# A two-layer diffusion block on one core: score matmuls in another order, FFN weights tied behind the attention's steps, down factors inside the up product, modulation and squares swapped

## The chip, the cores and the metric

The kernel runs on 1 core of a Trainium2 chip. The metric is the device time of one execution in microseconds (us). Before the change the median of 3 runs is 2509.74 us (2507.56 to 2510.74).

## What is computed

Two layers over 1024 latent tokens and 256 context tokens of width 1024. Each layer: RMS norm and modulation, one input projection, then windowed attention (8 query heads on 2 key heads, keys of the own block of 128 and its two neighbours, all 256 context keys and one sink per head) next to a Fourier mixing of 512 channels, an output projection, norm and gated residual; then norm and modulation again, a SwiGLU FFN of width 2816, norm and gated residual. Layer 1 updates the latent tokens alone. Cut to what matters here:

```python
mod_lat = silu(c) @ w_ada[i] + b_ada[i]                  # shifts, scales, gates, for latent
mod_ctx = silu(c_ctx) @ w_ada[i] + b_ada[i]              # and for context tokens
h = modulate(rmsnorm(x, norm_pre_mix[i]), sh1, sc1)
p = h @ w_in[i]                                          # q, k, v, u; q and k rotated
logits = concat([q @ k_window * scale + mask, q @ k_ctx * scale, sink])
attn = softmax(logits)[..., :-1] @ concat([v_window, v_ctx])
four = real(fft2(u)) @ w_four
x_mid = x + g1 * rmsnorm(concat([attn, four]) @ w_out[i])
hf = modulate(rmsnorm(x_mid, norm_pre_ffn[i]), sh2, sc2)
x = x_mid + g2 * rmsnorm((silu(hf @ w_gate[i]) * (hf @ w_up[i])) @ w_down[i])
```

## The kernel before

Activations lie transposed in the chip's memory (channels on the 128 partitions, tokens along the row), in two token blocks, A and B (640 tokens each in layer 0, 512 in layer 1). Every product is made of two-part numbers, three matmuls for one: in the projections and the attention in a 32-bit format, in the FFN in float16. The FFN's up product is done as seven half-size products for eight (a Strassen-Winograd form), so that each of the 22 weight matrices of 128 hidden columns (11 of gate, 11 of up) is first turned into sums of its quarters.

**Who sets the order.** The program is written as Python generators which yield after each piece of work; `mix` takes a next piece from the generator whose share done, relative to the number given beside it, is lowest. A larger number thus spreads a generator's steps more tightly. The order so written is a priority only: a scheduler with a model of time reorders each engine's instructions and hands out the buffers of the pools. On the chip each engine then executes its own queue in order. `high_priority(offset=AHEAD_OF)` lets maximum, exponential and casts of the attention go ahead of work that is written earlier.

**Attention.** `attn` steps through pairs of heads. `score` (L191) writes the logits of one head into a two-bank tile (pool `sc`, two such tiles): the sink's column, the window in high and low part with two triangular masks of 128x128, the context in two parts. VectorE takes the maximum (`ng`, L215), ScalarE the exponential with its sum (`A`, `su`, L216). `turn` transposes the result on TensorE (`tp`, L226), and ScalarE (L230) and VectorE (L231) split it; `value` (L234) takes the reciprocal of the sums (L238, 128x128 after a broadcast) and multiplies with V (`pv`, L244). Beside it run `fill` (remaining projections, Fourier, first half of the output projection), in layer 0 also `work` (modulation by matmuls, L568) and `early`: `norms` (squares of 8 weight matrices, L448) and `ahead`, which makes the float16 parts of these 8 matrices and stores them in memory (`wc`). `sums` (L456) does that: high part on ScalarE (`wa` or `ww`, L464), low part on VectorE (L465), sums of quarters on VectorE (`raw`, L476 to L479).

**FFN.** 44 matrices' products (`matrix`, L1084) in three parts of `mix`. First beside residual, norms and operands of block B (`side`), then beside `down_norms` (24 loads of the down weights and their squares, L1158 and L1159), then beside the modulation of the next layer for the first and second third (`mod(0, 1)`, products with reduction on VectorE, L645, loads `wm` on SyncE's queue) and the squares of its first weights. From the fifth matrix pair on, weights are fresh: loaded into the pool `raw` (four tiles), squared, made by `sums`, used for both blocks. L1088 to L1115 evacuate a matrix's banks; L1120 to L1132 scale and split the hidden values. Behind the up product `down_scale(0)` (L1164) makes the factors `dn` of the down weights for block A: VectorE (L1169 to L1173), TensorE and VectorE in `highest` (L602, L603, L605), VectorE (L409 to L411, L1175). The down product (L1215) needs its weights `wd` from ScalarE (L1207) and VectorE (L1208) with that factor. Layer 1's first projection runs beside norm statistics (`nps` L667, `nr` L679, `rps` L689) and scaling of block B.

## Time and profile before

| | us |
|---|---|
| median of 3 runs | 2509.74 |
| the profiled execution | 2504.05 |
| its span, first to last instruction | 2502.2 |
| TensorE busy in it | 2352.4 |
| VectorE busy | 1787.2 |
| ScalarE busy | 1344.7 |

The stages in the span: layer 0's attention about 130 to 535 us, its FFN 576 to 1113, its down product to 1422; layer 1's projection and attention 1422 to 1780, its FFN 1827 to 2244, its down product to the end. TensorE's busy time counts each matmul with its run through the array, modelled, and matmuls overlap; so the distance from start to start is the better measure of one. The granted clock is TensorE's, as a share of full speed. A row of a wait names who waits, on whom, us in total, how many times, and the longest.

### The profile page before, as it was taken

What the parts mean: (1) busy time and instruction counts of PE and PEld (TensorE: products, weight loads), DVE (VectorE), ACT (ScalarE), POOL (GpSimd) and SP (SyncE); (2) the same over time, 40 slices, a digit from 0 to 9 for tenths busy, and PEclk for the clock granted to TensorE, in tenths of its full rate; (3) what the DMA queues carried; (4) which work ended last, traced back from release to release, by engine and by line L of the source; (5) the groups of instructions that cost most, each with busy time, mean ns of one, the idle gap of its engine ahead of it and who ended that gap; (6) DMA issues with size and microseconds to landing.
All of it is one profiled execution on the core that took longest, in us unless ns stands there. A gap on an engine that the chain in (4) does not pass through costs nothing. (4 is left out here: it accounts for less than half of the span.)

```text
span 2502.2 us, 44066 instructions
## 1 busy us (share of the span) xinstructions
PE 2352.4 (94%) x17224; PEld 1900.2 (76%) x17224; DVE 1787.2 (71%) x3462; ACT 1344.7 (54%) x2587; POOL 196.6 (8%) x204
## 2 busy tenths in 40 slices
...
GB/s 309 206 102 167 160 98 107 184 236 284 203 185 148 108 129 165 156 192 373 269 246 129 91 123 47 35 18 51 186 338 222 161 72 69 77 142 208 132 254 125
DMA packets 157377, 406.83 MB, mean 163 GB/s; under 512 B 17488, under 2 KB 34288, under 8 KB 157168
## 3 DMA queue, kind: packets, MB, share of 16 engines
...
## 5 line engine op out<-in xcount | busy, mean ns | idle before, releaser
L1084 PE MATMUL p<-ffn,ww 128*128 128x320 f16 (+1 forms) x7392 | 921.9, 287 | 25.5 <-ACT ww L464 5.5
L1084 PEld LDWEIGHTS <-ww 128*128 128x128 f16 x7392 | 722.7, 98 | 220.8 <-issue 23.5
L1215 PEld LDWEIGHTS <-wd 128*128 128x128 f16 x3696 | 363.6, 99 | 164.0 <-ACT wd L1207 5.8
L1215 PE MATMUL acc<-hid,wd 128*128 128x320 f16 (+2 forms) x2544 | 335.4, 294 | 3.5 <-ACT wd L1207 3.2
L1208 DVE SCALAR_TENSOR_TENSOR wd<-raw,dn,wd 128x256 f16<-128x256 f32 x440 | 186.4, 480 | 132.6 <-ACT wd L1207 132.0
L1207 ACT ACTIVATE wd<-raw,dn 128x256 f16<-128x256 f32 x440 | 187.2, 496 | 146.0 <-PE acc L1215 87.2
L518 PE MATMUL accn<-arena,hi 128*128 128x320 f32 (+1 forms) x992 | 252.2, 327 | 5.6 <-DVE X L259 2.0
L518 PE MATMUL acc<-arena,hi 128*128 128x320 f32 (+2 forms) x928 | 209.0, 330 | 5.6 <-ACT X L1038 3.8
L1215 PE MATMUL acc<-X,wd 128*128 128x320 f16 (+1 forms) x1152 | 195.0, 331 | 0.9 <-ACT wd L1207 0.9
L518 PEld LDWEIGHTS accn<-arena,hi 128*128 128x128 f32 x992 | 173.2, 190 | 16.3 <-DVE arena L231 2.7
L518 PEld LDWEIGHTS acc<-arena,hi 128*128 128x128 f32 x928 | 154.8, 190 | 23.4 <-ACT X L1038 5.3
L518 PE MATMUL accn<-arena,lo 128*128 128x320 f32 (+1 forms) x496 | 159.8, 325 | 1.7 <-DVE lo L400 1.7
L674 POOL TENSOR_TENSOR nr<-nm,mhalf 128x5 f32<-128x5 f32 (+2 forms) x17 | 18.2, 1069 | 1708.0 <-DVE nm L673 1708.0
L465 DVE SCALAR_TENSOR_TENSOR ww<-raw,sp,ww 128x1024 f16<-128x1024 f32 x112 | 125.4, 1147 | 27.3 <-ACT ww L464 27.1
L464 ACT ACTIVATE ww<-raw,sp 128x1024 f16<-128x1024 f32 x112 | 109.9, 1033 | 59.4 <-DVE raw L479 51.0
L400 DVE TENSOR_TENSOR lo<-raw,hi 128x1024 fp32r<-128x1024 f32 x77 | 101.6, 1320 | 55.0 <-ACT hi L399 39.9
L230 ACT CAST arena<-tp 128x512 fp32r<-128x512 f32 (+1 forms) x184 | 96.6, 528 | 76.6 <-PE tp L226 74.2
L216 ACT ACTIVATE A<-score,ng 128x641 f32<-128x641 f32 (+2 forms) x144 | 106.6, 741 | 46.9 <-PE tp L226 30.1
L215 DVE TENSOR_REDUCE ng<-score 128x1 f32<-128x641 f32 (+2 forms) x144 | 106.3, 740 | 28.6 <-PE score L208 27.3
L518 PE MATMUL acc<-arena,lo 128*128 128x320 f32 (+2 forms) x464 | 125.0, 327 | 0.1
L399 ACT CAST hi<-raw 128x1024 fp32r<-128x1024 f32 x77 | 80.6, 1047 | 75.1 <-PE acc L518 28.7
L448 ACT ACTIVATE junk<-raw 128x1024 bf16<-128x1024 f32 x88 | 92.3, 1051 | 42.1 <-DMA raw<-in_wup 19.2
(231 smaller groups left out, 3724.4 us busy)
## 6 DMA issues: line engine op xcount, KB each, us to landing
...
```

Of the source, the lines that this page charges most:

```text
L215: nc.vector.tensor_reduce(self.ng[:, hs], sv, axis=AX.X, op=ALU.max, negate=True)
L216: nc.scalar.activation(p, sv, AF.Exp, bias=self.ng[:, hs], accum_out=self.su[:, hs])
L230: nc.scalar.copy(ph, tp[:, 0:256 * n])
L400: nc.vector.tensor_tensor(lo[:, 0:w], raw[:, 0:w], hi[:, 0:w].bitcast(F32), op=ALU.subtract)
L448: self.nc.scalar.activation(junk[:], raw[j][:], AF.Square, accum_out=self.ss[:, j, i:i + 1])
L464: nc.scalar.activation(hi, src, AF.Copy, scale=s)
L465: nc.vector.scalar_tensor_tensor(lo, src, s, hi, op0=ALU.mult, op1=ALU.subtract)
L518: self.nc.tensor.matmul(ps, wt[:, ks], xt[:, a:b], start=(k == 0 and i == 0), stop=(k == n - 1 and i == 2))
L1084: nc.tensor.matmul(ps, w[:, at:at + P], G[:, k, x, c, 0:h], start=(start and k + t == 0), stop=(k == KD // 2 - 1 and t == 2), skip_group_c ...
L1207: nc.scalar.activation(wt[:, 0, c], raw[:, c], AF.Copy, scale=r)
L1208: nc.vector.scalar_tensor_tensor(wt[:, 1, c], raw[:, c], r, wt[:, 0, c], op0=ALU.mult, op1=ALU.subtract)
L1215: nc.tensor.matmul(out, wt[:, e, k], xs[x][:, s, u:v], start=(f + s + i == 0), stop=(f == NP - 1 and s == 1 and i == 2))
```

## The change

Seven things, in one diff. In `score` the long products come first, then the context's, then the masks, then the sink. The reciprocal is taken of the 128x2 sums, and a copy broadcasts it. Each score notes its maximum and its exponential (`urgent`), and with `issue_after` the squares, the high parts with their store, the low parts and the quarter sums of FFN weights that are written beside the attention are put behind them in ScalarE's and VectorE's order; `sums` now yields between its parts, with a further step between load and first use. `down_scale(0)` is called inside the up product, ahead of the last matrix's third product, so that its squares must be complete by then. `mod(0)` stands in the FFN's second part where `down_norms` stood; `down_norms` stands in the third with `mod(1)`. In layer 1's first projection the statistics of block B get the weight 9 for 14. The pace of the early weights follows the new number of steps (12 for 8 beside the attention, 28 of 40 steps for 16 of 24 beside down).

```diff
@@ score
-        nc.tensor.matmul(s[:, 511 - w:512 - w], net.bf1[:], net.sink[:, self.l, hd:hd + 1], start=True, stop=True)
         if w:
             loc = s[:, 512 - w:512]
             ls = slice(C + P * self.k0, C + P * self.k1)
             nc.tensor.matmul(loc, q, net.KHI[g][:, ls], start=True, stop=False)
-            if n > 0:
-                nc.tensor.matmul(loc[:, 0:P], net.bf[:, 0:P], net.bf[:, P:2 * P], start=False, stop=False)
-            if n < NB - 1:
-                nc.tensor.matmul(loc[:, w - P:w], net.bf[:, 0:P], net.bf[:, 2 * P:3 * P], start=False, stop=False)
-            nc.tensor.matmul(loc, q, net.KLO[g][:, ls], start=False, stop=True)
+            nc.tensor.matmul(loc, q, net.KLO[g][:, ls], start=False, stop=False)
         nc.tensor.matmul(s[:, 512:512 + C], q, net.KHI[g][:, 0:C], start=True, stop=False)
         nc.tensor.matmul(s[:, 512:512 + C], q, net.KLO[g][:, 0:C], start=False, stop=True)
+        if w:
+            if n > 0:
+                nc.tensor.matmul(loc[:, 0:P], net.bf[:, 0:P], net.bf[:, P:2 * P], start=False, stop=(n == NB - 1))
+            if n < NB - 1:
+                nc.tensor.matmul(loc[:, w - P:w], net.bf[:, 0:P], net.bf[:, 2 * P:3 * P], start=False, stop=True)
+        nc.tensor.matmul(s[:, 511 - w:512 - w], net.bf1[:], net.sink[:, self.l, hd:hd + 1], start=True, stop=True)
...
         with net.tc.high_priority(offset=AHEAD_OF):
-            nc.vector.tensor_reduce(self.ng[:, hs], sv, axis=AX.X, op=ALU.max, negate=True)
-            nc.scalar.activation(p, sv, AF.Exp, bias=self.ng[:, hs], accum_out=self.su[:, hs])
+            top = nc.vector.tensor_reduce(self.ng[:, hs], sv, axis=AX.X, op=ALU.max, negate=True)
+            exp = nc.scalar.activation(p, sv, AF.Exp, bias=self.ng[:, hs], accum_out=self.su[:, hs])
+        net.urgent = top.ins, exp.ins
@@ value
-            nc.vector.reciprocal(self.out[:, 0].rearrange("p (h d) -> p h d", h=2), self.su[:].unsqueeze(2).broadcast_to([P, 2, HD]))
+            nc.vector.reciprocal(self.su[:], self.su[:])
+            nc.vector.tensor_copy(self.out[:, 0].rearrange("p (h d) -> p h d", h=2), self.su[:].unsqueeze(2).broadcast_to([P, 2, HD]))
@@ norms
-            self.start(l, i)
+            raw = self.load(l, i)
             yield
+            self.squares(l, i, raw)
@@ squares, behind
+            with self.behind(1):
+                self.nc.scalar.activation(junk[:], raw[j][:], AF.Square, accum_out=self.ss[:, j, i:i + 1])
...
+    def behind(self, e):
+        return self.tc.issue_after(self.urgent[e]) if self.urgent else nullcontext()
@@ sums
-        parts(0, raw[0][:])
-        parts(1, a22)
+        one = high(0, raw[0][:]), high(1, a22)
         yield
-        nc.vector.tensor_tensor(a22, a21, a22, op=ALU.add)
...
-        parts(2, raw[0][:])
+        for e in one:
+            low(*e)
+        with self.behind(0):
+            nc.vector.tensor_tensor(a22, a21, a22, op=ALU.add)
...
         yield
-        parts(3, raw[1][:])
+        two = high(2, raw[0][:]), high(3, raw[1][:])
+        yield
+        for e in two:
+            low(*e)
         yield
@@ ffn_up
+                if n == 2 and m == (1, NP - 1, 1):
+                    self.down_scale(0)
@@ program
-                mix((self.inproj(l, 0, (1, 0, 2, 3, 4, 5)), cost(6, KD, BW - C)), (side, 14))
+                mix((self.inproj(l, 0, (1, 0, 2, 3, 4, 5)), cost(6, KD, BW - C)), (side, 9))
...
-            mix((fill, FILL[l]), (self.attn(l, queries), ATT[l]), (work, 17), (early, 8 * AHEAD))
+            mix((fill, FILL[l]), (self.attn(l, queries), ATT[l]), (work, 17), (early, 12 * AHEAD))
+            self.urgent = None
...
-            mix((part(up, 14 * AHEAD - 7), 2 * AHEAD * one), (self.down_norms(l), 24))
-            mix((up, one * (44 - 4 * AHEAD)), (mod(0, 1), 64), (iter(()) if last else self.norms(l + 1), 2 * AHEAD))
-            self.down_scale(0)
+            mix((part(up, 14 * AHEAD - 7), 2 * AHEAD * one), (mod(0), 32))
+            mix((up, one * (44 - 4 * AHEAD)), (self.down_norms(l), 30), (mod(1), 32),
+                (iter(()) if last else self.norms(l + 1), 2 * AHEAD))
...
-                mix(down(0, 0, w, first), (part(pre, 4 * AHEAD), 4 * AHEAD), (side, 32))
+                mix(down(0, 0, w, first), (part(pre, 7 * AHEAD), 7 * AHEAD), (side, 32))
```

How this moves the instructions shows at three places; the lines are those of each kernel's own file.

ScalarE in layer 0's attention, before: a weight's high part (`wa`) stands between two exponentials (`A,su<-score`) of a pair, and elsewhere ahead of a cast (`arena_391<-tp`).

```order
L867 CAST qs<-X 64x2x128 x2
L216 ACTIVATE A,su<-score,ng 128x641
L230 CAST arena_391<-tp 128x256
L464 ACTIVATE wa<-raw,sp_111 128x512
L216 ACTIVATE A,su<-score,ng 128x641
L469 DMA wc<-wa 128x512
L399 CAST hi<-raw 128x1024
L838 COPY X<-accn 128x320
L230 CAST arena_391<-tp 128x512
L257 COPY pvl<-pv 64x128 x2
L464 ACTIVATE wa<-raw,sp_111 128x1024
L230 CAST arena_391<-tp 128x512
```

The same engine and stage in the changed kernel (L218 is the exponential, L233 the cast, L479 the high part):

```order
L218 ACTIVATE A,su<-score,ng 128x641
L233 CAST arena_391<-tp 128x256
L218 ACTIVATE A,su<-score,ng 128x641
L479 ACTIVATE wa<-raw,sp_111 128x1024 x2
L404 CAST hi<-raw 128x1024
L482 DMA wc<-wa 128x1024 x2
L233 CAST arena_391<-tp 128x512
```

The high parts now come two at a time, directly behind the second exponential of a pair.

VectorE at the end of layer 0's up product, before: the reduction `hx` for block A's factors stands behind the last matrix's evacuations and maximum (`hm`), and the factors `dn_118` behind those of block B.

```order
L1115 SCALAR_TENSOR_TENSOR A<-p_11396,inv_122,A 128x320
L1103 TENSOR_TENSOR A<-A,p_11397 128x320
L1107 SCALAR_TENSOR_TENSOR A<-A,inv_122 128x960
L1120 TENSOR_REDUCE hm<-A 128x1
L603 TENSOR_REDUCE hx<-fps 1x1
L1121 TENSOR_SCALAR hm<-hm 128x1
L1122 TENSOR_SCALAR he<-hm 128x1
L1123 TENSOR_SCALAR hp<-he 128x1
L1169 TENSOR_SCALAR dn_119<-he 128x11
L409 TENSOR_SCALAR pe<-fps 128x1
```

The same in the changed kernel (L628 is `hx`, L1202 the factors, L1116 the evacuation of the last matrix's second product, L1235 the down weights' low part):

```order
L1157 SCALAR_TENSOR_TENSOR hid<-A,hp,hid 128x1280
L423 TENSOR_TENSOR sq<-ss 128x8
L628 TENSOR_REDUCE hx<-fps 1x1
L1116 TENSOR_TENSOR A<-A,p_11437 128x320
L414 TENSOR_SCALAR pe<-fps 128x1
L415 TENSOR_SCALAR dback_120<-pe 128x1
L416 TENSOR_SCALAR dback_120<-pe 128x1
L1202 TENSOR_SCALAR dn_118<-dn_118,dback_120 128x11
L1235 SCALAR_TENSOR_TENSOR wd<-raw,dn_118,wd 128x256 x4
```

The factors and the first down weights are made ahead of most of the last matrix's evacuations. On TensorE the two small matmuls of `highest` stand ahead of the last 24 matmuls of the up product, of which the last 12 stand behind 40 of the down product. In layer 1 the second of them stays behind the up product.

VectorE at the 17th matrix of layer 0's up product, before (L645 is a modulation product, its second row reads the sum out):

```order
L1091 TENSOR_TENSOR A<-A,p_7985 128x320
L465 SCALAR_TENSOR_TENSOR ww<-raw,sp_111,ww 128x1024
L1100 TENSOR_TENSOR A<-A,p_7832 128x320
L409 TENSOR_SCALAR pe<-wsum 128x1
L645 ISA wm,half<-wm,c,bada 128x512
L645 ISA half 128x1
L1115 SCALAR_TENSOR_TENSOR A<-p_7831,inv_122,A 128x320
```

In the changed kernel (L670 the modulation product, L1116 the evacuation that was L1091):

```order
L1116 TENSOR_TENSOR A<-A,p_8112 128x320
L500 TENSOR_TENSOR raw<-raw 128x512
L670 ISA junk,mod_104<-wm,c,half 128x512
L670 ISA mod_104 128x1
L670 ISA wm,mod_104<-wm,c,half 128x512
```

Between the 16th and the 19th evacuation of this kind (one a matrix) 34 modulation products now stand, where 10 stood. From the 20th matrix on it is 28 over 22 matrices, and ScalarE has 24 squares of down weights there (L1159 before). In layer 1's projection, 24 of the 120 matmuls that followed `rps` now precede `nps`, and 24 more precede `rps`.

35 lines of the change are left out of this document (22 added, 13 removed).

## The prediction

> **What bounds the kernel now.** I read a table of stretches cut at the stage borders, then who waits for whom on TensorE, then the timeline where the table shows holes. The table (us from the span's start, length, busy time of each engine, granted clock, DMA share, GB/s):
>
> ```profile
> core 0: us, PE busy (x) PEld busy (x) DVE busy (x) ACT busy (x) POOL busy (x), PEclk, DMA share, GB/s
> 130.00:440.00 310.00, 274.63 (x1910) 241.75 (x1909) 254.94 (x470) 190.09 (x411) 58.72 (x68) 0.96 0.38 125
> 440.00:535.00 95.00, 90.22 (x650) 84.72 (x648) 65.55 (x116) 56.42 (x108) 4.24 (x4) 1.00 0.52 174
> 690.00:750.00 60.00, 60.00 (x444) 43.21 (x443) 18.41 (x32) 15.90 (x28) 0.00 (x0) 1.00 0.58 188
> 750.00:1113.00 363.00, 347.56 (x2511) 245.13 (x2509) 281.26 (x578) 174.48 (x274) 0.00 (x0) 0.99 0.43 140
> 1490.00:1780.00 290.00, 277.69 (x1950) 253.09 (x1949) 233.81 (x440) 179.57 (x401) 58.35 (x67) 0.99 0.14 44
> 1780.00:1870.00 90.00, 81.05 (x510) 66.68 (x509) 64.18 (x116) 65.43 (x125) 9.54 (x7) 0.96 0.86 307
> 1870.00:2240.00 370.00, 368.12 (x3381) 329.57 (x3380) 260.63 (x501) 185.49 (x322) 1.01 (x1) 1.00 0.37 123
> ```
>
> TensorE is the bound nearly everywhere; what can be won is its holes. Layer 0's attention (130 to 535) leaves PE idle for 35.4 + 4.8 = 40.1 us of 405, 9.9%, and at 0.96 clock loses 0.04 x 310 = 12.4 us more. Layer 1's attention (1490 to 1780), the same work without context queries, modulation matmuls and FFN weights beside it, leaves 12.3 of 290, 4.2%. Layer 0's FFN (750 to 1113) leaves 15.4, with VectorE at 77%, while in 690 to 750 PE has no hole and VectorE is 31% busy. The start of layer 1's FFN (1780 to 1870) leaves 9 of 90. The rest of that FFN (1870 to 2240) leaves 2.
>
> **Attention, layer 0: the queue behind the steps.** TensorE's longest sum of waits there, and one such wait with what ScalarE did before it (timeline; brackets are idle time and who ended it):
>
> ```profile
> PE score L197 <- ACT A L216: 11.2, 10, 2.3
> PE fc L1019 <- DVE arena L910: 3.8, 2, 3.4
> ```
> ```profile
> 194.60 1.15 ACT L464 ACTIVATE wa<-raw,sp 128x1024 f16<-128x1024 f32 x1 [2.31 <-DVE raw L479]
> 197.52 0.16 PE L197 MATMUL score<-sink,bf 128*128 128x1 bf16 x1 [2.32 <-ACT A L216]
> ```
>
> At 194.6 ScalarE had waited 2.31 us, at the head of its queue, for VectorE's sums of the FFN weight (raw, L479), then made that weight, and the exponential that frees the score's bank came behind it; TensorE stood 2.32 us. The change ties these weights behind the last exponential (ScalarE) or maximum (VectorE) and puts a step between the sums and the parts that need them. It adds no semaphore, only an order in each queue. Idle above layer 1's rate is 40.1 - 0.042 x 405 = 23 us. I put 60% of it down to this edit, 14 us: the 8 weights still go through the same two queues. Bounds 0 and 23. The clock: half of 12.4 would be 6; I take 4, since some of it coincides with the holes. The Trainium skill, "TensorE: Matmul & The Clock Gate", section "What's actually happening", has the clock halved only after an idle window of about 3.4 us; just one wait there is that long, so by that rule these 4 us would be nothing. The 0.96 beside waits of 2.3 us speaks against it.
>
> **The reciprocal** (both attentions). VectorE rows, the first two of 130 to 535, the third of 1490 to 1780:
>
> ```profile
> L238 DVE RECIPROCAL pvl<-su 128x128 f32<-128x128 f32 x38 | 36.0, 947 | 1.0 <-ACT A L216 0.5
> L259 DVE TENSOR_TENSOR X<-pvl,pv 128x128 f32<-128x128 f32 x39 | 11.0, 283 | 1.1
> L238 DVE RECIPROCAL pvl<-su 128x128 f32<-128x128 f32 x32 | 30.4, 949 | 0.7
> ```
>
> Each becomes a reciprocal of 128x2 and a copy of 128x128. Neither is in the trace. A reciprocal of 128x128 bounds the pair's sum from above (no gain); from below stands a single 128x128 operation, 0.283. I take 0.45, nearer to the lower since the first has 2 columns of 128: 0.5 saved, x40 = 20 us of VectorE's 320 in layer 0, x32 = 16 of 234 in layer 1. It counts only where TensorE waits for VectorE: 3 us in each layer (0 to 7).
>
> **The score's order.** One score of three blocks, and two 384-column matmuls in a steady stream, for scale:
>
> ```profile
> 1541.75 0.18 PE L197 MATMUL score<-sink,bf 128*128 128x1 bf16 x1
> 1541.79 0.42 PE L201 MATMUL score<-arena,qs 128*128 128x384 f32 x1
> 1542.05 0.23 PE L203 MATMUL score<-bf 128*128 128x128 bf16 x1
> 1542.12 0.22 PE L205 MATMUL score<-bf 128*128 128x128 bf16 x1
> 1542.14 0.42 PE L206 MATMUL score<-arena,qs 128*128 128x384 f32 x1
> 1542.40 0.28 PE L207 MATMUL score<-arena,qs 128*128 128x256 f32 x1
> 1542.52 0.28 PE L208 MATMUL score<-arena,qs 128*128 128x256 f32 x1
> 1542.64 0.31 PE L518 MATMUL accn<-arena,hi 128*128 128x320 f32 x1
> ```
> ```profile
> 1427.06 0.33 PE L518 MATMUL acc<-arena,lo 128*128 128x384 f32 x1
> 1427.23 0.51 PE L518 MATMUL acc<-arena,hi 128*128 128x384 f32 x2
> ```
>
> A 384-column matmul takes 0.17 from start to start in the stream, 0.26 in the score, twice: behind the one-column sink matmul and behind the short masks the wide weight's load stands uncovered, 0.09 each. With the long ones first there is one such place left, behind the sink, paid by whatever follows. The score now takes 1542.64 - 1541.75 = 0.89; in the new order 2 x 0.17 + 2 x 0.12 + 2 x 0.07 + 0.04 + 0.09 = 0.85. Saved 0.04, x64 latent scores a layer = 2.6 us; where TensorE is bound 2 a layer. Bounds 0 and 2 x 0.09 x 64 = 11.5 a layer. The same page of the Trainium skill, section "Step-by-step: what each phase is for", lets the next weights load while a matmul runs; taken as always hidden, this edit is worth nothing and the sum is 4 us smaller. The 0.26 against 0.17 decides for the rows.
>
> Layer 0's attention: 14 + 4 + 3 + 2 = 23. Layer 1's: 3 + 2 + 1 for the clock (0.99 of 290 loses 2.9) = 6.
>
> **Layer 1's first projection (weight 14 to 9).** TensorE's timeline:
>
> ```profile
> 1453.93 0.77 PE L830 MATMUL vps<-cst,vt 128*128 128x128 f32 x5 [2.26 <-ACT vt L825]
> 1456.85 2.29 PE L667 MATMUL nps<-cst,ssq 128*128 128x1 f32 x10 [2.15 <-DVE ssq L661]
> 1465.67 1.30 PE L689 MATMUL rps<-cst,nr 128*128 128x128 f32 x5 [6.53 <-DVE nr L679]
> ```
>
> The statistics of block B stand in TensorE's queue ahead of 120 matmuls that don't need them: 11 us of waits. In the new order 24 of those stand ahead of nps and 24 more ahead of rps, 48 x 0.17 = 8.2 us of cover. But block B's operands then still need VectorE, which is busy from 1434 on; I take 5 (0 to 8.2).
>
> **The factors of down.** TensorE's timeline at both ends of the up product (the last matmuls ahead, the first steady stream behind):
>
> ```profile
> 1111.67 1.80 PE L1084 MATMUL p<-ffn,ww 128*128 128x320 f16 x12
> 1121.14 7.05 PE L1215 MATMUL acc<-X,wd 128*128 128x320 f16 x35
> ```
> ```profile
> 2241.43 2.79 PE L1084 MATMUL p<-ffn,ww 128*128 128x256 f16 x24
> 2250.87 5.37 PE L1215 MATMUL acc<-X,wd 128*128 128x512 f16 x14
> ```
>
> The hole is 1121.14 - 1113.47 = 7.7 us and 2250.87 - 2244.22 = 6.7. In layer 0 the new order has the whole chain (L602, L603, L605, dn) ahead of the last 24 up matmuls, and 40 down matmuls ahead of the last 12: 7 gained. In layer 1 L605 stays behind the up product, and dn (L1175) behind the last maximum: 2.5. Together 9.5 (5 to 13).
>
> **Modulation and squares swapped.** Durations (ScalarE 1790 to 1865, then VectorE 760 to 1110), and what TensorE waits for in 535 to 690 and in 750 to 1113:
>
> ```profile
> L1159 ACT ACTIVATE raw<-raw 128x1024 f32<-128x1024 f32 x16 | 16.9, 1056 | 10.6 <-DMA raw<-in_wdown 10.0 <-DVE X L712 0.6
> L1159 ACT ACTIVATION_READ_ACCUMULATOR raw<-raw 128x1 f32 x24 | 4.5, 187 | 0.0
> L1159 ACT ACTIVATE raw<-raw 128x768 f32<-128x768 f32 x8 | 6.7, 839 | 6.5 <-DMA raw<-in_wdown 6.5
> L645 DVE CUSTOM_DVE_ANT_0 wm<-wm,c,bada 128x512 f32<-128x512 f32 x32 | 23.6, 748 | 5.5 <-DMA wm<-in_wada 3.8 <-issue 1.4
> L645 DVE DVE_READ_ACCUMULATOR2_ANT half<- 128x1 f32 x48 | 4.0, 83 | 0.0
> ```
> ```profile
> PE p L1084 <- ACT A L1088: 2.9, 1, 2.9
> PE p L1084 <- ACT ww L464: 5.5, 8, 1.1
> ```
>
> Out of the starts of both FFNs go 24 squares of up to 1.24 us (1.056 + 0.187), 30 us of ScalarE's 65 in 1780 to 1870, with 16.5 us of standing at the head of its queue for their loads (10.0 and 6.5). I take 3 in layer 0 (the one wait of 2.9) and 5 of 9 in layer 1: 8 (3 to 12). Out of layer 0's later stretch go 64 of 96 modulation products of 0.83, 53 us of 281; half of its 15.4 us of holes go with them: 8 (0 to 15).
>
> What comes in costs. An up matrix is 84 matmuls of 60/444 us, 11.35. VectorE's other work there is (281.26 - 96 x 0.83)/32 = 6.3 a matrix. The new VectorE order has 34 modulation products between the 16th and the 19th L1091 (one a matrix): 28 + 3 x 6.3 = 47 us for 34 of TensorE, 13 over. TensorE's open banks cover about half a matrix, so 8 (2 to 13). Their 32 loads of 256 KB and the two broadcasts of c move with them on SyncE, past the weight loads; the DMA share of 0.58 has room. The 24 squares and their loads now stand among the later matrices, ahead of bank evacuations on ScalarE and in the same four raw tiles as the fresh weights; ScalarE is 48% and 50% busy there (174/363, 185/370). I take 4 for both layers (0 to 60, below). The number and size of the weight copies' issues and the split of the down stage (28 of 40 steps for 16 of 24) stay: nothing, since TensorE has no wait on these weights beside the down product.
>
> Sum: -23 - 6 - 5 - 9.5 - 8 - 8 + 8 + 4 = -47.5. The profiled execution took 2504.05 (span 2502.2), 5.7 below the median of the three runs, 2509.74. From the profile 2456.5, from the median 2462.
>
> **Rivals.** (1) The weights beside attention only change their victim: behind the last exponential they stand ahead of the casts (L230) that TensorE's value products need. For it: of ScalarE's and VectorE's work only the reciprocals go. Against it, ScalarE's row in 130 to 535:
>
> ```profile
> L230 ACT CAST arena<-tp 128x512 fp32r<-128x512 f32 x70 | 40.9, 585 | 28.9 <-PE tp L226 27.1 <-ACT wa L464 0.8 <-PE pv L252 0.4
> ```
>
> It stands idle 27.1 us ahead of these casts, waiting for transposes: room for the weights. The 14 and 4 are lost: 2480. (2) Layer 0's attention comes all the way to layer 1's rate (23 instead of 14) and the pile of modulation is covered: 2462 - 9 - 8 = 2445. (3) Slower: each of the 48 moved squares stands in front of an evacuation that TensorE needs, or its late load holds the queue and the fresh weights behind it. Full price 48 x 1.24 = 60 in place of 4: 2518. It ends above 2509.7 from (47.5 + 4)/48 = 1.1 us a square on. For it: in 1790 to 1865 such squares made ScalarE wait 16.5 us for loads. Against it: all waits of 750 to 1113, where 28 other squares stand, come to 15.4, at most 0.55 each. (4) The swap gives nothing, since pile and late squares eat its 16: 2466, inside the forecast.
>
> **How the numbers follow.** Forecast (with 4) 0.57, own range 2449 to 2476; (1) 0.21; (2) 0.15; (3) 0.07. The range 2436 to 2490 leaves out (3) and the far ends of (1) and (2). About 0.2%, 5 us, is what a measurement of this kernel can tell from no change. Slower 0.06 and within 0.04 come from (3) and from (1) with the pile in full; faster 0.90.
>
> **What would show it.** Idle PE in layer 0's attention 22 to 28 us instead of 40, waits on L216 under 6, clock 0.98; the small reciprocal and copy under 0.5 together; scores 0.04 shorter; nps and rps under 5 us of waits; no hole over 3 us at layer 0's down; about 8 us of idle PE at the 16th to 19th matrix behind L645; layer 1's 1780 to 1870 with 4 us idle. The forecast is wrong if the attention's holes stay (1), or if squares stand in front of waits over 1 us in the later matrices (3).

## The result, and the profile after

The changed kernel takes **2571.47 us** (median of 4 executions, 2566.61 to 2573.67) beside 2508.65 for the kernel before (4 executions, 2503.57 to 2510.74). The ratio is 1.0251, 95% interval 1.0229 to 1.0273: 63 us slower, where 47 us faster was forecast, and outside the range of 2436 to 2490. The profiled execution has a span of 2568.2 us, 66.0 more than before.

Where did they go? The plainest reading is to take events that both programs have, in the same order, and to subtract their times: the k-th matmul of the attention's transposes (tp), of the up product (p), of the down product (d), with k counted from 0. The first column of numbers is the kernel before, in us from the start of its span; the next is how much later the changed kernel gets there. The other columns belong to experiments below (1, 2, 3, 4, 13 and 14).

```
event                             before  change   e1     e2     e3     e4    e13    e14
tp 16    layer 0, attention start   144.2  +21.4  +14.0   +1.2  +21.9  +3.1   +2.1   +2.4
tp 40                               177.3  +27.9  +21.5   +8.2  +28.0  +5.0   +3.1   +4.2
tp 320   layer 0, attention's end   489.4  +22.9  +15.9   -1.5  +22.2  -0.4   -1.7   -6.3
p 0      layer 0, FFN               576.4  +24.6  +19.0   +1.3  +24.1  +4.3   +1.2   -2.0
p 1344   its 17th matrix            769.3  +24.4  +20.6   +2.5  +25.9  +5.1   -0.4   -0.6
p 2016   its 25th                   867.7  +48.5  +34.5  +24.5  +24.7  +6.0  +18.7   +2.5
p 3360   its 41st                  1066.3  +62.3  +32.1  +38.8  +31.9  +6.4  +17.6   -0.8
d 168    layer 0, down product     1150.8  +60.9  +30.0  +36.7  +31.1  +4.8  +15.1   -2.9
d 504                              1196.4  +70.8  +36.7  +45.1  +42.3  +7.0  +15.1   -1.6
d 1847   late in layer 0's down    1386.2  +75.1  +41.3  +53.4  +47.3  +8.6  +12.7   -4.1
tp 400   layer 1, attention        1562.9  +71.4  +36.1  +50.1  +43.8  +5.0   +7.8   -7.2
tp 639   its end                   1765.1  +66.0  +30.7  +44.7  +38.4  -0.3   +2.4  -12.6
p 4032   layer 1, FFN's start      1872.9  +60.0  +24.7  +38.6  +38.0  -2.6   -3.7  -18.6
p 7391   its end                   2244.0  +64.2  +30.2  +45.3  +37.9  -2.6   +2.7  -13.1
d 3695   the end                   2484.2  +66.3  +31.4  +46.5  +39.2  -1.0   +3.7  -11.8
```

Layer 1 went much as forecast: 75.1, which still stands at layer 0's last down matmul (1422.1 before, 1497.1 changed), falls to 71.4 over the projection, to 66.0 over the attention, to 60.0 at the FFN's start. Everything is lost in layer 0, in three places: 28 us by transpose 40 (5 of them come with the four small edits alone, column e4), 24 between the 17th and the 25th up matrix, some 27 from there until late in the down product. Of the 23 us that the attention should have won, 5 are there (27.9 to 22.9).

**The first 100 to 190 us.** TensorE's clock and idle time, before and in the changed kernel (table of stretches, columns as in the prediction):

```profile
100.00:130.00 30.00, 29.59 (x194) 25.13 (x191) 15.14 (x24) 22.77 (x46) 1.47 (x2) 1.00 0.82 279
130.00:160.00 30.00, 25.32 (x161) 23.89 (x160) 24.96 (x51) 24.26 (x60) 7.86 (x10) 0.89 0.28 89
160.00:190.00 30.00, 28.25 (x197) 22.43 (x196) 23.58 (x49) 17.70 (x43) 6.38 (x8) 1.00 0.28 89
```
```profile
100.00:130.00 30.00, 22.19 (x132) 20.03 (x134) 6.12 (x15) 15.73 (x33) 1.47 (x2) 0.83 0.59 193
130.00:160.00 30.00, 19.79 (x97) 15.46 (x93) 15.83 (x31) 21.20 (x46) 2.70 (x3) 0.72 0.39 131
160.00:190.00 30.00, 25.64 (x154) 22.93 (x153) 19.76 (x49) 19.30 (x45) 6.51 (x8) 0.83 0.42 137
```

Idle PE rises from 6.8 to 22.4 us, by 15.6, and the clock takes as much again: 0.17 x 30 + 0.28 x 30 + 0.17 x 30 = 18.6 us lost instead of 3.3. The longest wait and what leads to it, in the changed kernel's timeline (SyncE's queue, ScalarE, TensorE; the number behind the engine is the line):

```profile
73.17 0.81 SPq L446 DMA_DIRECT2D raw<-in_wgate  x2
75.56 0.81 SPq L446 DMA_DIRECT2D raw<-in_wup  x2
...
101.08 0.34 SPq L564 DMA_DIRECT2D wada<-in_wada  x1
102.12 0.33 SPq L401 DMA_DIRECT2D raw<-in_win  x1
```
```profile
99.45 0.48 ACT L218 ACTIVATE A<-score,ng 128x257 f32<-128x257 f32 x1
...
99.92 1.04 ACT L454 ACTIVATE junk<-raw 128x1024 bf16<-128x1024 f32 x1
...
106.37 1.04 ACT L404 CAST hi<-raw 128x1024 fp32r<-128x1024 f32 x1 [4.28 <-DMA raw<-in_win]
```
```profile
107.47 0.90 PE L543 MATMUL acc<-arena,hi 128*128 128x320 f32 x2 [8.51 <-ACT hi L404]
```

Four loads of FFN weights at 73 to 76 us take all four raw tiles. Their squares stand behind the attention's exponentials, at 99.9; only then are tiles free, the tiles for the modulation (wada) and the projection's next weight (in_win) at 101 and 102. The weight arrives at 106, and TensorE has stood 8.5 us. Before, that load went out at 93.35 (in the kernel with the four small edits alone, experiment 4, at 96.34):

```profile
73.97 18.38 SPq L440 DMA_DIRECT2D raw<-in_wup  x2
...
93.35 0.38 SPq L396 DMA_DIRECT2D raw<-in_win  x1
```

**Layer 0's attention.** TensorE's waits in 348 us of equal work (the changed kernel's stretch lies 25 us later), before and changed:

```profile
PE score L197 <- ACT A L216: 9.6, 7, 2.3
...
PE v L955 <- DVE arena L910: 2.8, 3, 1.9
```
```profile
PE ada L593 <- DMA wada<-in_wada: 4.8, 4, 2.5
PE v L980 <- DVE arena L935: 3.9, 2, 3.7
PE tp L229 <- DVE PTX L234: 3.8, 2, 2.2
...
PE score L201 <- ACT A L218: 2.9, 5, 1.0
```

The wait for the exponential did fall, from 9.6 to 2.9. In its place stand loads that found no tile (wada) and VectorE's low parts of transposes (PTX, arena), behind two low parts of a weight in one piece:

```profile
332.92 2.97 DVE L487 SCALAR_TENSOR_TENSOR wa<-raw,sp,wa 128x1024 f16<-128x1024 f32 x2
...
336.25 0.69 DVE L234 TENSOR_TENSOR PTX<-tp,arena 128x512 fp32r<-128x512 f32 x1
```

The table of stretches gives an idle PE of 348 - 317.15 = 30.9 us there instead of 348 - 313.23 = 34.8, and the clock is 0.96 instead of 0.97.

**The pile in layer 0's FFN.** The four sums of one fresh weight on VectorE (timelines, before and changed; before, nothing stands between the sums; the rows left out in the changed kernel are modulation products, L670, and evacuations):

```profile
767.11 0.69 DVE L476 TENSOR_TENSOR raw<-raw 128x512 f32<-128x512 f32 x1
...
769.28 0.69 DVE L479 TENSOR_TENSOR raw<-raw 128x512 f32<-128x512 f32 x1
```

```profile
791.40 0.68 DVE L497 TENSOR_TENSOR raw<-raw 128x512 f32<-128x512 f32 x1
792.00 0.74 DVE L670 CUSTOM_DVE_ANT_0 junk<-wm,c,half 128x512 f32<-128x512 f32 x1
...
793.35 0.68 DVE L498 TENSOR_TENSOR raw<-raw 128x512 f32<-128x512 f32 x1
...
795.69 0.68 DVE L499 TENSOR_TENSOR raw<-raw 128x512 f32<-128x512 f32 x1
...
798.04 0.68 DVE L500 TENSOR_TENSOR raw<-raw 128x512 f32<-128x512 f32 x1
...
803.39 1.27 DVE L487 SCALAR_TENSOR_TENSOR ww<-raw,sp,ww 128x1024 f16<-128x1024 f32 x1
```

Sums that take 2.7 us of work last from 791.4 to 798.7, where before they lasted from 767.1 to 770.0, and the last low part ends at 804.7. Until then the weight keeps its two raw tiles, so that the next weight's loads, squares, factor and sums all start late. Table of stretches with equal work, from the 1176th up matmul or a little later to the 2016th, before and changed:

```profile
754.00:868.00 114.00, 108.52 (x794) 77.06 (x793) 92.15 (x203) 58.30 (x93) 0.00 (x0) 1.00 0.42 138
```
```profile
778.00:916.00 138.00, 119.08 (x793) 81.13 (x791) 94.24 (x201) 60.52 (x97) 0.00 (x0) 0.91 0.42 137
```

The 24 us are made up of some 18.9 - 5.5 = 13.4 of idle PE and some 0.09 x 138 = 12.4 of clock. In the changed kernel's stretch TensorE waits 12.0 us for weights and their norms and 6.9 for ScalarE's evacuations. VectorE has hardly more to do than before (94.24 and 92.15): it is the order that costs.

**From there on.** Waits of 770 to 1185 in the changed kernel:

```profile
ACT raw L1186 <- DMA raw<-in_wdown: 24.7, 19, 3.6
...
PE p L1109 <- ACT ww L479: 18.3, 10, 4.5
...
PE p L1109 <- ACT A L1124: 12.8, 9, 2.3
...
PE wsum L425 <- DVE sq L423: 8.5, 6, 3.5
```

The late squares (L1186) wait for their loads at the head of ScalarE's queue, 24.7 us in all, with evacuations (A) and weights (ww) behind them. TensorE's waits for weights, evacuations and norms (the 18.3, 12.8 and 8.5) were 5.5, 2.5 and 1.5 in 750 to 1113 before. In the down product (1180 to 1300) the parts of layer 1's early weights wait once 8.5 us for a load which went out at 1209.2: on SyncE's queue it stood behind 14 loads of hidden values (hid, 1194.9 to 1207.5) and two stores. The down weights' parts (wd) stand behind them.

```profile
DVE wa L487 <- ACT wa L479: 13.7, 5, 11.2
ACT wa L479 <- DMA raw<-in_wup: 9.1, 2, 8.5
...
PE acc L1242 <- ACT wd L1234: 5.1, 3, 3.6
```

### The profile page after: what moved, and what is told of

The parts are those of the page before. It is cut to its first block, busy times and chain, and to the rows that moved or that the text cites. A ratio compares the mean times of both kernels' runs of the same rounds, so it can differ in the third digit from the quotient of the medians.

```text
span 2568.2 us, 44194 instructions
## 1 busy us (share of the span) xinstructions
PE 2373.9 (92%) x17224; PEld 1913.1 (74%) x17224; DVE 1751.0 (68%) x3534; ACT 1347.8 (52%) x2587; POOL 196.5 (8%) x204
## 5 line engine op out<-in xcount | busy, mean ns | idle before, releaser
L1109 PE MATMUL p<-ffn,ww 128*128 128x320 f16 (+1 forms) x7392 | 940.8, 290 | 50.5 <-ACT ww L479 20.3
L1235 DVE SCALAR_TENSOR_TENSOR wd<-raw,dn,wd 128x256 f16<-128x256 f32 x440 | 185.9, 480 | 98.2 <-ACT wd L1234 96.9
L233 ACT CAST arena<-tp 128x512 fp32r<-128x512 f32 (+1 forms) x184 | 97.0, 530 | 91.6 <-PE tp L229 86.4
L479 ACT ACTIVATE ww<-raw,sp 128x1024 f16<-128x1024 f32 x112 | 110.4, 1033 | 51.5 <-DVE raw L500 39.1
L218 ACT ACTIVATE A<-score,ng 128x641 f32<-128x641 f32 (+2 forms) x144 | 106.8, 742 | 47.7 <-PE tp L229 28.0
L686 DVE TENSOR_TENSOR ssq<-ssq,sq 128x640 f32<-128x640 f32 (+2 forms) x119 | 87.4, 734 | 58.9 <-ACT sq L685 56.3
```

What stands on the lines that cost most here:

```text
L218: exp = nc.scalar.activation(p, sv, AF.Exp, bias=self.ng[:, hs], accum_out=self.su[:, hs])
L233: nc.scalar.copy(ph, tp[:, 0:256 * n])
L479: nc.scalar.activation(hi, src, AF.Copy, scale=s)
L686: nc.vector.tensor_tensor(s[:, 0:w], s[:, 0:w], t[:, 0:w], op=ALU.add)
L1109: nc.tensor.matmul(ps, w[:, at:at + P], G[:, k, x, c, 0:h], start=(start and k + t == 0), stop=(k == KD // 2 - 1 and t == 2), skip_group_c ...
L1235: nc.vector.scalar_tensor_tensor(wt[:, 1, c], raw[:, c], r, wt[:, 0, c], op0=ALU.mult, op1=ALU.subtract)
```

## The experiments

The line numbers in the diffs' code are left out; "changed" and "before" say which kernel was edited. All ratios are against the kernel before, run beside each.

**1. Load and squares in one step** (changed).

```diff
 def norms(self, l):
     for i in range(2 * AHEAD):
-        raw = self.load(l, i)
+        self.start(l, i)
         yield
-        self.squares(l, i, raw)
```

> The changed kernel with one edit undone: the 8 pairs of FFN weights whose squares are taken during the first attention steps are again loaded and squared in one step, instead of loaded one step ahead of their squares. Theory S (four raw tiles): the 25 us that the changed kernel loses between 100 and 180 us come from two such pairs holding all four raw tiles until their squares, while the projection's next weight (raw<-in_win) waits for a tile; then the first context score with long rows comes at 160 to 168 us again instead of 187 and the time falls by 15 to 25 us, to 2547 to 2556. Rival Q (queue): the loss comes from the squares standing behind the exponentials on ScalarE; then this edit gives back less than 5 us, 2566 to 2572. In both theories the FFN of layer 0 stays as slow as in the changed kernel (first to last up matmul 606 us, before 537... 1113.2 - 576.4; changed 1176 - 601 = 575).

2532.12 us, 1.0089 (1.0064 to 1.0114): 39 less than the changed kernel. The size was a miss, and so was the place: column e1 wins 7 us by the end of the first attention (4 of them are left at the 17th up matrix), 27 more between that matrix and the down product, and 3 in it. The early weights of layer 1 are squared there by the same lines, which I had not counted. Loading one step ahead of the squares is what costs in the FFN; in the first 100 to 190 us most of the loss stays, so theory S has the smaller part of it.

**2. Nothing tied behind the attention's steps** (changed).

```diff
 def behind(self, e):
-    return self.tc.issue_after(self.urgent[e]) if self.urgent else nullcontext()
+    return nullcontext()
```

> The changed kernel with nothing tied behind the last exponential or maximum (the order of steps, the split of sums and parts and all else as in the changed kernel). Theory Q: the stretch 100 to 190 us wins back 15 us or more. Theory S: it wins less than 8 us there, since the loads still run a step ahead of their squares. Inside the attention (from 190 on) the waits of the score for the exponential rise again from 3 to 8 us or more and the waits for VectorE's casts of transposes fall. Forecast by S: 2562 to 2578.

2549.70 us, 1.0157 (1.0129 to 1.0185): 22 less, outside what S forecast. The loss of the attention's start is gone (+1.2 at transpose 16 instead of +21.4), as theory Q said: without the tie the early load brings none of it. The waits for the exponential did not rise again, as was expected (3.5 us from 190 to 535), so their fall in the changed kernel does not need the tie.

**3. Modulation and squares back in their places** (changed).

```diff
-mix((part(up, 14 * AHEAD - 7), 2 * AHEAD * one), (mod(0), 32))
-mix((up, one * (44 - 4 * AHEAD)), (self.down_norms(l), 30), (mod(1), 32),
+mix((part(up, 14 * AHEAD - 7), 2 * AHEAD * one), (self.down_norms(l), 24))
+mix((up, one * (44 - 4 * AHEAD)), (mod(0, 1), 64),
```

> The changed kernel with modulation and squares in their old places (24 squares of the down weights beside the first matrices' later half, 64 modulation products later); the down factor of block 0 stays inside the up product. My theory: the swap costs layer 0's FFN 575 - 537 = 38 us, of which some 7 are the down factor's own hole, and it wins 4 to 6 at the start of layer 1's FFN: the time falls by 28 to 42 us, to 2530 to 2544. Rival: the loss in layer 0's FFN is in the split of sums and parts of its weights (which this kernel keeps); then the time falls by less than 10.

2543.70 us, 1.0139 (1.0118 to 1.0160): 28 less, as expected, and the 24 us between the 17th and the 25th matrix are gone (+25.9 to +24.7). Layer 1 gives its 6 us at the FFN's start back (38.4 to 38.0 instead of 66.0 to 60.0) and saves the 4 later: even.

**4. The four small edits alone** (before): reciprocal, score order, statistics at weight 9, block 0's down factor inside up.

```diff
-nc.vector.reciprocal(self.out[:, 0]..., self.su[:].unsqueeze(2).broadcast_to([P, 2, HD]))
+nc.vector.reciprocal(self.su[:], self.su[:])
+nc.vector.tensor_copy(self.out[:, 0]..., self.su[:].unsqueeze(2).broadcast_to([P, 2, HD]))
...
-mix((self.inproj(l, 0, (1, 0, 2, 3, 4, 5)), cost(6, KD, BW - C)), (side, 14))
+mix((self.inproj(l, 0, (1, 0, 2, 3, 4, 5)), cost(6, KD, BW - C)), (side, 9))
...
+if n == 2 and m == (1, NP - 1, 1):
+    self.down_scale(0)
...
-self.down_scale(0)
 places = self.hidden(l, blocks)
```

> The kernel before with four of the edits alone: the reciprocal of two columns and a copy, the score with its long products first, layer 1's statistics at weight 9, block 0's down factor inside the up product. By the terms of the prediction: reciprocal 6, score 4, clock 1, projection 5, down factor 9.5, together 25 us under the kernel before, 2484. By what the changed kernel's trace shows of layer 1 (attention 6 shorter, projection 3): 2486 to 2492. Rival: the reciprocal and the score gain only in company of the other edits; 2495 or more.

2494.28 us, 0.9946 (0.9928 to 0.9964): 14 faster than before, of the 25 in the prediction's terms: slower than the 2484 and the 2486 to 2492 that were expected, and just under the rival's 2495. Its nine executions lie between 2486.8 and 2502.9, and the profiled one is the slowest of them, so column e4 is to be read by the change from row to row: layer 0's attention -3.5 (after +3.1 at its start), layer 1's projection -3.6, its attention -5.3.

**5. The modulation's loads on another queue** (changed).

```diff
 raw = self.tmp.tile([P, 512], F32, tag="t", name="wm")
-nc.sync.dma_start(raw[:], self.io["wada"][l, a, h, k][:, 512 * w:512 * w + 512])
+nc.gpsimd.dma_start(raw[:], self.io["wada"][l, a, h, k][:, 512 * w:512 * w + 512])
```

> The changed kernel with the 96 loads of the modulation matrix (wm<-in_wada, 256 KB each) issued on GpSimd's queue instead of SyncE's. In the changed kernel layer 0's FFN loses 24 us between its 1344th and 2016th up matmul (769 to 868 us before), where the modulation products pile up. Theory Y (SyncE's queue): the products hold the tiles that the next modulation loads wait for, those loads stand in SyncE's queue at 785 to 801 and 805 to 822 us, and the loads of the next gate and up weights stand behind them until 803; then with the loads on another queue the loss between these two matmuls falls from 24 to 12 us or less and the time by 10 to 20, to 2551 to 2562. Rival V (VectorE): the products themselves delay VectorE's sums, parts and bank evacuations; then the loss stays at 20 or more and the time at 2565 to 2575.

2585.19 us, 1.0314 (1.0287 to 1.0341): slower still, and above both forecasts. Theory Y falls. SyncE now stands free from 785 on, and the next weight's load still goes out only when VectorE's last low part has freed a raw tile:

```profile
782.61 1.91 SPq L1160 DMA_DIRECT2D hs<-hid  x2
803.59 2.92 SPq L446 DMA_DIRECT2D raw<-in_wup  x2
```

The loss between the 17th and the 25th matrix is 32 us here. It is VectorE's pile, through the raw tiles, and not SyncE's queue. Why the time is 14 us longer than the changed kernel's is not shown.

**6. Short squares for the early weights** (changed; only where norms takes them).

```diff
-self.nc.scalar.activation(junk[:], raw[j][:], AF.Square, ...)
+self.nc.scalar.activation(junk[:, 0:8], raw[j][:, 0:8], AF.Square, ...)
```

> The changed kernel, where the squares of the 8 early weights of each layer (beside layer 0's first attention steps, and beside layer 0's later up matrices for layer 1) are taken over 8 columns instead of 1024, so that these sums leave out the other columns; loads, tiles and order stay. It takes 32 x 1.0 us from ScalarE. Putting load and squares back in one step gave 39 us in the run before this one, 7 of them in the first attention and 31 after it. Theory S (tiles and queue order): the price is the early load, which holds two of four raw tiles from one step to the next, and the place of the squares in ScalarE's queue behind what they wait for; then the time falls by less than 14 us, to 2557 to 2571. Rival T (ScalarE's time): the squares themselves delay the evacuations behind them; then most of the 39 comes back, 2532 to 2545.

2575.30 us, 1.0262 (1.0233 to 1.0290), beside 1.0251 for the changed kernel: 32 us less of ScalarE bring nothing (theory S had allowed up to 14). Rival T falls. The squares cost by where they stand, with the loads that they need and the tiles that they keep, and not by their duration.

**7. Edits 1, 2 and 3 undone together** (changed; the three diffs above in one kernel).

> The changed kernel with the three edits undone that cost most in the runs so far: load and squares of the early weights in one step, nothing tied behind the exponential, modulation and squares in their old places. What remains are the four small edits (2494 alone), the split of sums and parts, the paces of the early weights, and the load one step ahead of the sums. If these three explain the loss in layer 0, the time is the small edits' 2494 plus up to 10 us that the changed kernel loses in the first quarter of layer 0's down product (SyncE's and ScalarE's queue, early weights of layer 1): 2492 to 2506. If the split and the paces cost more: 2510 or over.

2523.24 us, 1.0065 (1.0042 to 1.0087): 48 less than the changed kernel, but 29 over the small edits, where I had left 10 at most. Something that I had priced at nothing costs 20 or more. What is left in this kernel are the split of sums and parts, the loads of the early weights one step ahead, and the paces. Undone singly the three edits gave 39, 22 and 28, together 48 and not 89: they cost through each other.

**8. The small edits, and late squares in layer 1 alone** (before).

```diff
-mix((part(up, 14 * AHEAD - 7), 2 * AHEAD * one), (self.down_norms(l), 24))
-mix((up, ...), (mod(0, 1), 64), (iter(()) if last else self.norms(l + 1), 2 * AHEAD))
+mix((part(up, 14 * AHEAD - 7), 2 * AHEAD * one), (iter(()) if last else self.down_norms(l), 24))
+mix((up, ...), (mod(0, 1), 64), (self.down_norms(l), 30) if last else (self.norms(l + 1), 2 * AHEAD))
```

> The kernel before with the four small edits, and with the 24 squares of the down weights moved to the later matrices in layer 1 alone, where no modulation and no early weights stand beside them. In the changed kernel the start of layer 1's FFN became 6 us shorter and its later part and the down product 4 to 6 us longer. By the prediction's terms (5 saved at the start, 2 lost later): 3 us under the small edits alone, 2491. If the late squares cost what they cost in the changed kernel: no difference, 2494. If they cost only in company of the other loads: 2488.

2494.49 us, 0.9950 (0.9930 to 0.9969): no difference from experiment 4. The squares win at the start of layer 1's FFN what they cost later.

**9. The split of sums and parts alone** (experiment 4's kernel).

```diff
-parts(0, raw[0][:])
-parts(1, a22)
+one = high(0, raw[0][:]), high(1, a22)
 yield
+for e in one:
+    low(*e)
 ...
-parts(2, raw[0][:])
 yield
-parts(3, raw[1][:])
+two = high(2, raw[0][:]), high(3, raw[1][:])
+yield
+for e in two:
+    low(*e)
 yield
...
-(early, 8 * AHEAD)   (part(pre, 4 * AHEAD), 4 * AHEAD)
+(early, 10 * AHEAD)  (part(pre, 5 * AHEAD), 5 * AHEAD)
```

> The kernel before with the four small edits (2494 alone) and the split of the FFN weights' work: first two high parts, a step, two low parts and the sums, a step, two high parts, a step, two low parts, where before each low part came right behind its high part. The loads stay in one step with the first parts, nothing is tied behind the exponential, the paces are set for four steps a weight. The run with three edits undone was 2523, 29 over the small edits. Theory W (split): the split puts pairs of low parts (2.5 us) on VectorE and pairs of high parts (2.1 us) on ScalarE in one piece, and each weight gives its raw tiles back later; it carries most of the 29: 2508 to 2522, with layer 1's FFN, whose code is otherwise that of the small edits, 3 or more us longer. Rival L (early load): it costs under 6, 2490 to 2500, and the next run carries the cost.

2512.04 us, 1.0013 (0.9996 to 1.0029): 18 over experiment 4. Layer 1's FFN is no longer than there: 5.7 us behind experiment 4's profile at its start and 5.7 at its end, so that part of theory W is wrong. Nor do the tiles come back later. From the issue of a weight's first load to the end of its last low part, the mean over the 8 early weights is 35.1 us beside layer 0's attention and 30.2 beside its down product; in experiment 4 it is 36.7 and 31.8. The 18 us are measured, but longer holding does not explain them. The pace of 10 for 8 also moves the early work: the last square starts at 148 us instead of 159, the first high part at 169 instead of 191. That a part of the 18 belongs to the pace is not excluded.

**10. The early weights' loads one step ahead alone** (experiment 4's kernel).

```diff
 for i in range(2 * AHEAD):
-    yield from self.sums(l, i, self.load(l, i), out, True)
+    raw = self.load(l, i)
+    yield
+    yield from self.sums(l, i, raw, out, True)
...
-(early, 8 * AHEAD)   (part(pre, 4 * AHEAD), 4 * AHEAD)
+(early, 10 * AHEAD)  (part(pre, 5 * AHEAD), 5 * AHEAD)
```

> The kernel before with the four small edits and with the loads of the early FFN weights one step ahead of their sums (the sums themselves as before, the paces set for the added step). Rival L: two of the four raw tiles are held a step longer while the loads of the projection's and the down product's weights wait for a tile; it carries most of the 29 us: 2508 to 2522, most of it in the first half of layer 0's down product and beside layer 0's attention. Theory W: under 6, 2490 to 2500.

2509.25 us, 0.9999 (0.9985 to 1.0013): 15 over experiment 4. Neither theory has it alone: 18 and 15 come near the 29 of experiment 7, and each just about eats the small edits' gain. Here the tiles are held longer, as rival L said, 40.5 and 33.1 us, and the pace is that of experiment 9 (last square at 150, first high part at 171).

**11. The tie alone, without the squares** (experiment 4's kernel; the four sums are tied as the low parts are): what the prediction priced at 14 us.

```diff
-nc.scalar.activation(hi, src, AF.Copy, scale=s)
-nc.vector.scalar_tensor_tensor(lo, src, s, hi, op0=ALU.mult, op1=ALU.subtract)
+with self.behind(1):
+    nc.scalar.activation(hi, src, AF.Copy, scale=s)
+with self.behind(0):
+    nc.vector.scalar_tensor_tensor(lo, src, s, hi, op0=ALU.mult, op1=ALU.subtract)
...
```

> The kernel before with the four small edits and with the early FFN weights' parts and sums (not the squares) tied behind the last exponential on ScalarE and the last maximum on VectorE. It is the largest term of the prediction alone. As the prediction had it: 14 us off layer 0's attention, 2480. By the changed kernel's trace (waits for the exponential fall from 10 to 3 us, waits for VectorE's casts and for loads rise by as much): no gain, 2490 to 2498, and no delay between 100 and 180 us, since that came with the squares. If the tie itself delays the start: 2505 or more.

2493.59 us, 0.9938 (0.9915 to 0.9960), beside 0.9946 (0.9928 to 0.9964): no gain that can be told from none, and no delay. Within layer 0's attention there is a gain: 348 - 320.88 = 27.1 us of idle PE in 187 to 535 instead of 348 - 313.22 = 34.8 in experiment 4, and waits for the exponential of 2.2 us instead of 6.7. The tied weights keep their raw tiles for 46.6 us instead of 36.7. Here, then, tiles held 10 us longer cost nothing.

**12. The tie of the squares alone** (experiment 4's kernel).

```diff
-self.nc.scalar.activation(junk[:], raw[j][:], AF.Square, accum_out=self.ss[:, j, i:i + 1])
+with self.behind(1):
+    self.nc.scalar.activation(junk[:], raw[j][:], AF.Square, accum_out=self.ss[:, j, i:i + 1])
```

> The kernel before with the four small edits (2494 alone) and with only the squares of the early FFN weights tied behind the last exponential on ScalarE. Theory Q: in the first attention steps a square then waits for an exponential that itself waits for the projection, its two raw tiles stay taken, and the projection's next weight, whose load waits for a raw tile, comes late: the first transposes come 8 us or more later, the attention starts 10 us or more later, and the time is 2504 to 2515. Rival: the tie needs the load a step ahead to cost anything; then 2490 to 2498.

2510.54 us, 1.0014 (1.0000 to 1.0028): 16 over experiment 4, without any early load, so that rival falls. The second half of a pair of loads now waits from 74.8 to 97.4 for a tile (in experiment 4 to 95.3), and the projection's weights are late from there on (SyncE's queue, then ScalarE's waits between 95 and 190):

```profile
74.82 0.37 SPq L445 DMA_DIRECT2D raw<-in_wup  x1
97.43 0.34 SPq L445 DMA_DIRECT2D raw<-in_wup  x1
98.47 0.33 SPq L401 DMA_DIRECT2D raw<-in_win  x1
```
```profile
ACT hi L404 <- DMA raw<-in_win: 7.8, 4, 3.6
```

In experiment 4 this wait is 2.4, in the changed kernel 12.0. TensorE's idle time in that stretch rises from 7.7 us (experiment 4) to 16.3, and the clock falls from 0.93 to 0.87. Theory Q has the time and the direction, but not the size of the delay: beside column e4, transpose 16 comes 0.4 us later, transpose 40 6.7 and the FFN 5.3, where it had 8 and 10. Some 7 of the 16 us stand elsewhere in this profile: layer 1's FFN takes 424.6 us from its first to its last up matmul, 417.8 in experiment 4. Its code is the same in both, but ScalarE's and VectorE's instructions stand in another order there, so the edit reached it through the scheduler. The tie of the squares is needed for the 21 us that the changed kernel loses by transpose 16 (experiment 2), but alone it does not bring them.

**13. The swap alone** (experiment 4's kernel, with the lines that experiment 3 took out).

```diff
-mix((part(up, 14 * AHEAD - 7), 2 * AHEAD * one), (self.down_norms(l), 24))
-mix((up, one * (44 - 4 * AHEAD)), (mod(0, 1), 64), (iter(()) ...
+mix((part(up, 14 * AHEAD - 7), 2 * AHEAD * one), (mod(0), 32))
+mix((up, one * (44 - 4 * AHEAD)), (self.down_norms(l), 30), (mod(1), 32), (iter(()) ...
```

> The kernel before with the four small edits and with modulation and squares swapped as in the changed kernel, in both layers; early weights and their loads as before. The prediction's terms for the swap come to -8 - 8 + 8 + 4 = -4: 2490. By the changed kernel's stretches the pile of modulation products at layer 0's 16th to 20th matrix costs 15 to 24 us, the late squares in layer 0 up to 7, and layer 1 comes out even: 2510 to 2522.

2511.54 us, 1.0017 (1.0004 to 1.0029): 17 over experiment 4, as expected, where the prediction's terms had -4. Column e13, row by row: the pile +19.1 (-0.4 to +18.7, where experiment 4 has +0.9); the later up matrices -1.1 (experiment 4: +0.4); layer 1's FFN start -6.1 (2.4 to -3.7; experiment 4 -2.3), the rest of that FFN +6.4.

**14. Experiments 8 and 11 together.**

> The kernel before with the four small edits, the early weights' parts and sums tied behind the attention's exponential and maximum, and the down weights' squares late in layer 1 alone. The two additions gave nothing that could be told from zero, each alone (2493.6 and 2494.5 beside 2494.3). If they add nothing together: 2490 to 2498. If the gains seen in their profiles (5 us in layer 0's attention, 6 at the start of layer 1's FFN) hold: 2484 to 2490.

2491.48 us, 0.9938 (0.9924 to 0.9953): faster than the kernel before by 0.6%, and the fastest here, though not by more than the intervals from experiment 4; it lies where the two additions add nothing. In its profile layer 0's attention has 348 - 321.23 = 26.8 us of idle PE (27.1 in experiment 11, 34.8 in the kernel before and in experiment 4), TensorE waits 2.2 us for exponentials instead of 9.6, and the clock is 0.96:

```profile
187.00:535.00 348.00, 321.23 (x2254) 290.24 (x2253) 267.68 (x534) 211.49 (x432) 50.66 (x59) 0.96 0.44 147
```

## Why the prediction was wrong, by its own steps

Put together from the medians, each part alone on top of the four small edits' 2494.3:

```
four small edits                     2508.5 -> 2494.3   -14    (terms of the prediction: -25.5)
+ weights tied behind the steps                          -1    (-14 and -4 for the clock)
+ squares tied behind the exponential                   +16    (not priced)
+ split of sums and parts                               +18    (at nothing)
+ early weights' loads a step ahead                     +15    (not priced)
+ modulation and squares swapped                        +17    (-4)
sum 2494.3 + 65 = 2559; the changed kernel 2571.5
```

Experiment 4's own interval is about 4.5 us to each side, so each difference is uncertain by some 5 us. The 12 us left over were not tried alone: the loads a step ahead of the squares (39 us in company, experiment 1), the paces, and what these edits do to each other. Since undone singly three of the edits gave 89 us and together 48, it is in part luck that the sum comes so near.

**The step that failed** is "It adds no semaphore, only an order in each queue", and with it "the number and size of the weight copies' issues and the split of the down stage ... stay: nothing". The prediction took an order, a split and an earlier load as free as long as TensorE had no wait on the moved work itself. The squares' tie was not priced at all, nor the step of loading ahead of them, and the split of each weight's sums and parts was not named there but taken into the tie. What stands in its place: where an instruction stands also decides when the raw tiles that it reads come free, and five users load into the same four: the early weights, the projection's weights, the modulation's (wada), the gate and up weights, the down weights. The prediction has these tiles once, for the late squares in the FFN.

How far this is shown differs by edit. For the tied squares the rows show the projection's weight going out late for want of a tile (102.1 instead of 93.4 in the changed kernel, 98.5 instead of 96.3 in experiment 12), though only 5 to 7 of experiment 12's 16 us stand there. For the pile, SyncE stood free and the next load waited until 803.6 for VectorE's last low part (experiment 5). For the split and the early load the cost is measured, 18 and 15 us, and the path is open: the split holds no tile longer, while the tie of the weights holds them 10 us longer and costs nothing (experiments 9 and 11). Two rivals were not separated from them: the faster pace, and the scheduler, which after such an edit also reorders stages whose code did not change (experiment 12). No run gave the pool a fifth tile, which would be the direct test.

**The tie of the weights, 14 us.** The mechanism was right in kind and the size was not: the wait for exponentials falls from 6.7 to 2.2, and layer 0's attention has 8 us less of idle PE (experiments 4, 11 and 14). At the end -1 is left by the medians, with the uncertainty above. That is near to rival (1)'s "only change their victim". The victims are the modulation's loads (wada, 4.5 us in experiment 14) and VectorE's low parts of transposes, and not the casts on ScalarE that rival (1) named, whose idle row I used against it. Rival (1) had .21; its 2480 was too fast by all that it took over from the other terms.

**The clock, 4 us.** Not there: 0.96 in the changed kernel's attention and in experiment 14's, although the long waits for exponentials are gone. Read in windows of 4 us, experiment 14's clock is 1.00 but for five stretches, in which it falls to 0.50 (in one to 0.71), and each stands behind a wait of TensorE: 2.7 and 1.7 us close together (at 316 and 319), 3.7 (337), 1.8 (354), 2.9 (380) and 2.3 (526). Four of them cost 3.4 us each, one 1.7. As long as waits of this size are left, for whatever engine, the clock term stays. The Trainium skill, "TensorE: Matmul & The Clock Gate", "What's actually happening", gave 0 for this term, which is what came, but its idle window of about 3.4 us is not what is seen: only one of these waits is that long, and in 130 to 160 the changed kernel was granted 0.72 with no wait over 2.9 us.

**The pile: 8, measured 18** (19.1 - 0.9 in experiment 13). VectorE's 13 us of overload was right as far as it went. By the rows it went further because each weight's sums are strung out between the products, its tiles come free late, and the next weight's whole chain starts late. The clock then about doubled the holes, 13.4 and 12.4 us in the changed kernel.

**The late squares: 4, with a rival of 60.** Rival (3) had the right place and sign, with .07, but not the price: alone (experiments 8 and 13) 4.5 and 6.4 us in layer 1, which the gain of 6 at the FFN's start pays; nothing to be seen in layer 0. The rival's stop was to be 1.1 us a square; the losses that made the kernel slower were others.

**Half of the later holes, -8.** 1.1 us won in experiment 13, where experiment 4 loses 0.4.

**The starts of the FFNs, -8.** Layer 0's 1.6 (p 0 to p 1344: 1.2 to -0.4, where experiment 4 has +0.8, so 2.4 by difference) for 3; layer 1's 6 in the changed kernel, 3.8 by difference in experiment 13, for 5. Right.

**Reciprocal and score.** The pair takes 0.16 + 0.25 = 0.41 us where 0.45 was taken; VectorE rows of the changed kernel's layer 0 attention, and a three-block score in its layer 1 (compare 0.89 before):

```profile
L242 DVE COPY pvl<-su 128x128 f32<-128x128 f32 x30 | 7.6, 254 | 0.3
L241 DVE RECIPROCAL su<-su 128x2 f32<-128x2 f32 x29 | 4.6, 159 | 4.0 <-ACT A L218 3.8
```
```profile
1599.10 0.42 PE L201 MATMUL score<-arena,qs 128*128 128x384 f32 x1
1599.36 0.34 PE L202 MATMUL score<-arena,qs 128*128 128x384 f32 x1
1599.54 0.29 PE L203 MATMUL score<-arena,qs 128*128 128x256 f32 x1
...
1599.91 0.17 PE L210 MATMUL score<-sink,bf 128*128 128x1 bf16 x1
1599.94 0.39 PE L543 MATMUL accn<-arena,hi 128*128 128x320 f32 x1
```

1599.94 - 1599.10 = 0.84 us (0.85 in the sum; the median over the scores without a wait is 0.82). The one long load left stands behind the sink, 0.26 from L201 to L202, and 0.18 to the next: as read. So a score became 0.04 to 0.07 shorter for 0.04. Layer 1's attention became 5.4 us shorter for 6 forecast; the reciprocal and the score were not run apart. In layer 0 experiment 4 wins 3.5 between transposes 16 and 320, for 3 + 2, but is +3.1 at the one and +4.3 at the FFN's start, so that nothing is left of it there. The load of the next weights taken as always hidden, as in the Trainium skill, "TensorE: Matmul & The Clock Gate", "Step-by-step: what each phase is for", would have made the score's edit nothing; the 0.26 and 0.18 say otherwise.

**Projection, -5:** 3.7 in the changed kernel, 3.6 and 5.1 in experiments 4 and 8 (1386.2 to 1562.9). Right. **Down factors, -9.5:** mis-sized. From the last up matmul on, layer 0 wins 1.4 in experiment 4 and 3.0 in experiment 8, for 7; layer 1 1.8 and 2.7, for 2.5, but its down product then takes 3.4 and 4.1 longer, which is not explained. In layer 0 the factor's end stands behind block 1's own evacuation and maximum on VectorE (experiment 8: the matmul that it needs starts at 1118.00, dn at 1121.29), and TensorE has a hole after all:

```profile
1118.63 1.22 DVE L1109 SCALAR_TENSOR_TENSOR A<-A,inv 128x960 f32<-128x960 f32 x1
...
1119.89 1.48 DVE L1122 TENSOR_REDUCE hm<-A 128x1 f32<-128x1280 f32 x1
1121.29 0.22 DVE L1179 TENSOR_SCALAR dn<-dn,dback 128x11 f32<-128x11 f32 x1
```
```profile
1122.11 16.10 PE L1219 MATMUL acc<-X,wd 128*128 128x320 f16 x96 [3.73 <-ACT wd L1211]
```

What stays open: how the 12 us left over divide, and where in the span and by what path the split and the early load lose their 18 and 15 us. Layer 1's FFN has experiment 4's order of instructions in both, up to a row or two, and takes 418.1 and 419.0 us for 417.8, so the loss lies ahead of it. Executions of one of these kernels lie 3 to 19 us apart, and experiments 4 and 8, with the same order of instructions in layer 0, differ by 7 us in its down product, so that single profiles do not place losses of this size.
